# A fused transformer layer on one core: first attention with some transfers issued from ScalarE's queue, other buffers and another unit order

## The chip, the cores and the metric

The kernel runs on one core of a Trainium2 chip. The metric is the device time of one execution in microseconds. Below, PE is TensorE, PEld its weight loads, DVE VectorE, ACT ScalarE, POOL GpSimd, and SP SyncE, which in this kernel issues every DMA. A DMA is issued by an instruction in one engine's own queue and is done when its data has landed.

## What is computed

The reference is one transformer layer in float32 on 1024 tokens of width 1024: a feed-forward part, a token mixer, a second feed-forward part and a last norm. The change lies in the token mixer:

```
proj = h @ w_in                      # queries, keys, values, gates
y_da = diff_attention(q_da, k_da, v_da, ...)   # 8 heads, two components each
y_ns = nsa(q_ns, kc, vc, ks, vs, kw, vw, ...)  # 16 heads: compressed, selected, window
merged = sigmoid(g_a) * (y_da @ w_proj_da) + sigmoid(g_b) * (y_ns @ w_proj_nsa)
```

`diff_attention` rotates queries and keys, takes two causal softmaxes p0 and p1 of 64-wide components, forms a = p0 - lam * p1, multiplies by the 128-wide values of the head, and applies an RMS norm to each head's result.

## The kernel before, in words

Every matrix product of the projections is done with high and low halves: `split` (line 85) writes the rounded high half on ACT and the remainder on DVE, and `mm3` (line 48) does three matmuls, high by high, low by high, high by low.

`mix` (line 1107) calls `prelim` (line 1139), `da_phase` (line 1223) and `ns_phase` (line 1284). All three draw on **units**, generators of one projection each:

- `rope_pair` (line 531) makes a pair of 128-wide column blocks of queries or keys, both blocks of 512 tokens in turn (the index tb). It rotates them (tiles `m13`, `m42`), splits them into `rh` and `rl`, and stores them to DRAM scratch (line 553): queries as high, low, high, keys as high, low. The pool `mp` holds one buffer for each of these four tags.
- `v_da_unit` (line 561) makes the values of one head: gemm, transposes, split into `vh` and `vl`, two stores (line 576). `vh` takes the buffer of tag `rh`, `vl` that of `rl`.
- `cmp_block` (line 747) is the compressed attention; it runs for the second attention's queries inside the four units u = 0 to 3 at the end of `prelim`, and ends in the stores of line 780.

`prelim` makes the raw columns, compressed keys and values, values of heads 0 and 1, then the four units with `cmp_block`, and closes its pools. `da_phase` opens pools for keys `dk` (B_DK = 4 buffers), values `dv` and queries `dq` (4 buffers) and then drains six units: queries and keys of heads 0 and 1 (pair 0), then queries, keys and two value units of pair 1, with head 0's keys and values loaded between them by `da_load_parts` (line 900) and the first queries loaded before the last unit.

Then come 8 heads h with 4 steps m each. `da_queries` (line 801) loads the queries of a step: two tiles, four DMAs (line 808). `da_scores` (line 814) computes, for two 128-row blocks z of the step and both components c, the scores S (line 789; 128 (i + 1) columns for row block i = 2m + z), mask and row maximum on DVE (line 796), and the exponential into `Pt` on ACT (line 798). S has two buffers in PSUM. `finish` of the step before transposes and splits the weights (`tr_split`, tiles `th` and `tl`, line 844), multiplies by the values (`da_pv`, lines 866 to 868) and, for every second step, normalizes: `da_finish2` (line 880) works in tiles `yr` and `zr`, writes both halves `yo` of the result into the same two tags and stores them (line 893). A head's keys are two tiles `kt`, loaded at line 906, its values two tiles `vt`, line 913.

Beside the heads runs a **filler** (`Filler`, line 1030): the units of pairs 2 and 3, gate units and, in the second attention, output projections. After each row block `step` hands out its share of gemms; the weights are loaded at line 1055 and split at lines 1065 and 1066.

Each engine works through its own list in order. The lists are laid down when the kernel is built, from the program's order, which sets the priorities, and a simulated timeline (line 1564); a DMA issue stands in the list of the engine that issues it, and an instruction whose semaphore is not there yet holds all that stand behind it in that list.

Of the kernel before, what the change touches and what calls it, by code (L numbers as in the profile page):

```python
# [7 lines left out]
F32 = mybir.dt.float32  # L8
F32R = mybir.dt.float32r
# [521 lines left out]
def rope_pair(K, c, scr, cmp=None):  # L531
    nc = K.nc
    w = [load_w(K, K.A["win"][c]), load_w(K, K.A["win"][c + 1])]
    for tb in range(NTB):
# [17 lines left out]
        for hl, t in ((0, rh), (1, rl), (2, rh))[:scr.shape[0]]:  # L552
            nc.sync.dma_start(out=scr[hl].rearrange("a s d t -> (s d) a t")[:, :, sl], in_=t.bitcast(F32))
        if cmp is not None:
            uh = K.mq.tile([P, 2, TB], F32R, tag="uh", name="uh")
            ul = K.mq.tile([P, 2, TB], F32R, tag="ul", name="ul")
            split(nc, uh, ul, uf)
            cmp(tb, uh, ul)


def v_da_unit(K, h):
    nc = K.nc
    w = load_w(K, K.A["win"][C_VDA + h])
    for tb in range(NTB):
        ps = K.gm.tile([P, TB], F32, tag="gm", name="gm")
        yield from fill_gemm(K, ps, w, K.h[tb])
        vt = K.mp.tile([P, TB], F32, tag="m13", name="vt")
        nc.vector.tensor_tensor(out=vt, in0=ps, in1=K.R[tb], op=ALU.mult)
        tr = K.gm.tile([P, 4, P], F32, tag="gm", name="tr")
        for j in range(4):  # L570
            nc.tensor.transpose(tr[:, j], vt[:, j * P:(j + 1) * P], K.ident)
        vh = K.mp.tile([P, 4, P], F32R, tag="rh", name="vh")
        vl = K.mp.tile([P, 4, P], F32R, tag="rl", name="vl")
        split(nc, vh, vl, tr)
        for hl, t in ((0, vh), (1, vl)):
            nc.sync.dma_start(out=K.s_v[h][hl][:, tb * 4:tb * 4 + 4], in_=t.bitcast(F32))

# [222 lines left out]

def da_queries(K, h, m):
    nc = K.nc
    qt = []
    p, s0 = h // 2, (h % 2) * 2
    for c in range(2):
        t = K.qp.tile([P, 2, 2 * P], F32R, tag="q", name="qt")
        for z in range(2):
            nc.sync.dma_start(out=t[:, z].bitcast(F32),
                              in_=K.s_q[p][z:z + 2, :, s0 + c, :, m * 256:(m + 1) * 256].rearrange("h a d t -> (h a) d t"))
# [70 lines left out]
def da_finish2(K, h, H, ob, sq):  # L880
# [8 lines left out]
    nc.vector.scalar_tensor_tensor(out=ob, in0=ob, scalar=K.hgain[:, h:h + 1], in1=y, op0=ALU.mult, op1=ALU.mult)  # L889
    yo = [K.op.tile([P, TB], F32R, tag=t, name="yo") for t in ("yr", "zr")]  # L890
    split(nc, yo[0], yo[1], ob)
    for i in range(2):
        nc.sync.dma_start(out=K.s_yda[H][h][:, i], in_=yo[i].bitcast(F32))

# [244 lines left out]
def prelim(K, cg):  # L1139
    nc, A = K.nc, K.A  # L1140
    K.gm = open_pool(K, cg, "gm0", 4, True, side="right")
    with ExitStack() as ctx:
# [30 lines left out]
        with ExitStack() as c2:  # L1173
# [14 lines left out]
            drain([v_da_unit(K, 1)])  # L1188
        for u in range(4):
            drain([rope_pair(K, C_QNS + 2 * u, K.s_qns[u], lambda tb, uh, ul, u=u: cmp_block(K, u, tb, uh, ul))])  # L1190

# [14 lines left out]
B_ST = 2  # L1206
B_DK = 4
B_DV = 2
# [14 lines left out]
def da_phase(K, cg):  # L1223
    nc = K.nc
    with ExitStack() as ctx:
        K.kp, K.vp, K.qp = open_pool(K, ctx, "dk", B_DK), open_pool(K, ctx, "dv", B_DV), open_pool(K, ctx, "dq", B_DQ)
        K.nk, K.vv = {}, {}
        for n, f in enumerate(da_units(K, 0)[:2] + da_units(K, 1)):
            if n == 2:
                early = da_load_parts(K, 0)  # L1230
            if n >= 2:
                next(early)
            if n == 5:
                q0 = da_queries(K, 0, 0)
            drain([f()])
        cg.close()
        K.low = LOW_DA
# [28 lines left out]
        for p in range(4):  # L1266
            fill.pace(4 * (p + 1) if p < 2 else 8 + ng * (p - 1), PACE_DA)
            for h in (2 * p, 2 * p + 1):
                if h:
                    da_load(K, h)  # L1270
                for m in range(4):
                    qt = q0 if h + m == 0 else da_queries(K, h, m)
                    if h == 4:
                        ns_load_key(K, m)
                    res = da_scores(K, h, m, qt, fill.step)
                    if pend:
# [113 lines left out]
def body(tc, A, out):  # L1390
    nc = tc.nc
    K = Ctx()
    K.tc, K.nc, K.A = tc, nc, A
    K.low, K.vv, K.gate, K.fill, K.seen = 0, {}, None, None, {}
    K.h, K.acc, K.R = [None] * 2, [None] * 2, [None] * 2
# [173 lines left out]
```

## Time and profile before

| what | value |
|---|---|
| median of 3 runs | 2980.08 us (2974.42 to 2980.65) |
| the profiled execution's own time | 2971.48 us |
| its span, first to last instruction | 2969.7 us |
| mean granted TensorE clock | 0.992 of full speed |
| PE busy | 2860.9 us (96%) |
| DVE, ACT, POOL busy | 1981.6 (67%), 1268.5 (43%), 971.5 us (33%) |
| DMA | 478.19 MB, 161 GB/s, 46.5% of 16 engines' time, all from SP's queue |

By stage, in us from the span's start: first feed-forward part 0 to 650, `prelim` 650 to 980, first attention 980 to 1490, second attention 1490 to 2100, projections to 2230, second feed-forward part to the end.

How to read it: "busy" counts an instruction from start to end; matmuls overlap, so a stretch with PE busy throughout is fed, not necessarily at its peak. The number in square brackets at the end of a timeline row is the idle time just before it and what ended that. PEclk in a table of stretches is the granted clock, 1.00 for 2.4 GHz and 0.50 for 1.2 GHz.

### The profile page before, as it was taken

What the parts mean: (1) busy time and instruction counts of PE and PEld (TensorE: products, weight loads), DVE (VectorE), ACT (ScalarE), POOL (GpSimd) and SP (SyncE); (2) the same over time, 40 slices, a digit from 0 to 9 for tenths busy, and PEclk for the clock granted to TensorE, in tenths of its full rate; (3) what the DMA queues carried; (4) which work ended last, traced back from release to release, by engine and by line L of the source; (5) the groups of instructions that cost most, each with busy time, mean ns of one, the idle gap of its engine ahead of it and who ended that gap; (6) DMA issues with size and microseconds to landing.
All of it is one profiled execution on the core that took longest, in us unless ns stands there. A gap on an engine that the chain in (4) does not pass through costs nothing.

```text
span 2969.7 us, 39965 instructions
## 1 busy us (share of the span) xinstructions
PE 2860.9 (96%) x14238; PEld 2390.4 (80%) x14238; DVE 1981.6 (67%) x3140; ACT 1268.5 (43%) x2195; POOL 971.5 (33%) x765
## 2 busy tenths in 40 slices
PE   8999999999999899989899999999999999999998
PEld 6887887888788678778778888888878888788886
DVE  8765666666687467667677777776333866667656
ACT  6322234443233245445566666666432522223443
POOL 4356651000144123222333233333242435664101
PEclk9999999999999999999999999999999999999999
DMA  4345458655456544544332234222742245455854
GB/s 139 113 167 195 155 188 309 215 182 167 153 201 219 185 163 158 180 166 163 113 119 84 86 114 162 77 83 78 290 153 93 71 145 177 164 190 203 290 182 148
DMA packets 212710, 478.19 MB, mean 161 GB/s; under 512 B 20896, under 2 KB 39584, under 8 KB 212512
## 3 DMA queue, kind: packets, MB, share of 16 engines
q1 hardware_dynamic: 212512, 475.65, 46.5%
q8 instruction: 112, 1.84, 0.2%
q14 instruction: 86, 0.70, 0.1%
HBM read 313.56 MB, written 162.00 MB: 160 GB/s over the span
## 4 chain that ended last, share of the span: by engine, by line
PE 67%; DMA 10%; DVE 6%; issue 4%; ACT 3%; POOL 2%; SPq 1%; DVEq 0%; ACTq 0%; POOLq 0%
PE gm L49 6%; PE S L789 6%; PE gm L50 6%; PE gm L51 6%; PE Y L324 5%; PE acc L49 5%; PE acc L51 5%; PE acc L50 5%; PE tr L844 4%; PE Z L324 4%; PE X L324 3%; PE o L1002 2%; PE o L1001 2%; DMA sg<-smx 2%; DVE wlo L82 1%
## 5 line engine op out<-in xcount | busy, mean ns | idle before, releaser
L49 PE MATMUL gm<-hi,whi 128*128 128x512 f32 x880 | 351.3, 399 | 4.1 <-ACT whi L86 1.7
L51 PE MATMUL gm<-hi,wlo 128*128 128x512 f32 x880 | 347.7, 396 | 1.0 <-DVE wlo L82 1.0
L50 PE MATMUL gm<-lo,whi 128*128 128x512 f32 x880 | 348.0, 395 | 0.0
L789 PE MATMUL S<-kt,qt 128*128 128x320 f32 (+5 forms) x1152 | 275.3, 353 | 35.9 <-ACT Pt L798 11.3
L82 DVE TENSOR_TENSOR tl<-tr,th 128x512 fp32r<-128x512 f32 (+2 forms) x384 | 236.2, 619 | 88.1 <-ACT th L86 84.5
L86 ACT ACTIVATE th<-tr 128x512 fp32r<-128x512 f32 (+2 forms) x384 | 203.7, 542 | 197.4 <-PE tr L844 193.8
L82 DVE TENSOR_TENSOR wlo<-st,whi 128x1024 fp32r<-128x1024 f32 x154 | 198.7, 1308 | 116.9 <-ACT whi L86 116.1
L324 PE MATMUL Y<-tf,whi 128*128 128x512 f32 x864 | 269.9, 394 | 4.4 <-DVE c L367 1.8
L796 DVE CUSTOM_DVE_ANT_0 S<-S,slab 128x896 f32<-128x896 f32 (+7 forms) x320 | 224.5, 709 | 65.5 <-PE S L789 59.8
L49 PE MATMUL acc<-whi 128*128 128x512 f32 (+1 forms) x628 | 242.8, 387 | 3.8 <-DVE u L398 3.8
L50 PE MATMUL acc<-wlo,whi 128*128 128x512 f32 (+1 forms) x628 | 242.8, 387 | 0.0
L51 PE MATMUL acc<-whi,wlo 128*128 128x512 f32 (+1 forms) x628 | 242.7, 388 | 0.0
L86 ACT ACTIVATE whi<-st 128x1024 fp32r<-128x1024 f32 x154 | 160.3, 1057 | 192.4 <-PE acc L51 109.7
L955 POOL TENSOR_SCALAR Ps<-Ps,l 128x384 f32<-128x384 f32 (+7 forms) x128 | 100.8, 788 | 426.0 <-DVE l L953 212.6
L789 PEld LDWEIGHTS S<-kt,qt 128*128 128x128 f32 x1152 | 183.5, 190 | 60.7 <-ACT Pw L798 13.2
L82 DVE TENSOR_TENSOR wlo<-a,whi 128x1024 fp32r<-128x1024 f32 x90 | 136.6, 1522 | 96.4 <-ACT whi L86 96.3
L49 PEld LDWEIGHTS gm<-hi,whi 128*128 128x128 f32 x880 | 168.0, 191 | 37.1 <-issue 2.0
L51 PEld LDWEIGHTS gm<-hi,wlo 128*128 128x128 f32 x880 | 167.7, 191 | 37.5 <-DVE wlo L82 1.7
L324 PEld LDWEIGHTS Y<-tf,whi 128*128 128x128 f32 x864 | 161.3, 188 | 45.0 <-issue 4.2
L50 PEld LDWEIGHTS gm<-lo,whi 128*128 128x128 f32 x880 | 167.8, 191 | 30.8
L324 PE MATMUL Y<-tf,wlo 128*128 128x512 f32 x432 | 169.4, 393 | 0.0
L1001 PE MATMUL o<-th,vt 128*128 128x256 f32 (+1 forms) x608 | 164.4, 287 | 1.8 <-ACT th L86 1.7
(314 smaller groups left out, 7007.5 us busy)
## 6 DMA issues: line engine op xcount, KB each, us to landing
wst<-in_win_dram SPq DMA_DIRECT2D x55, 512.0 KB
sw<-w2s SPq DMA_DIRECT2D x44, 512.0 KB
st<-sw SPq DMA_DIRECT2D x88, 256.0 KB
st<-saT SPq DMA_DIRECT2D x88, 256.0 KB
a<-in_f1w_dram SPq DMA_DIRECT2D x36, 512.0 KB
a<-in_f2w_dram SPq DMA_DIRECT2D x36, 512.0 KB
st<-saB SPq DMA_DIRECT2D x66, 256.0 KB
qt<-sq SPq DMA_DIRECT2D x128, 128.0 KB
```

The costliest lines, as they stand in the source:

```text
L49: first = nc.tensor.matmul(out, lhsT=w[0][:, wk], rhs=x[0], start=start, stop=False, skip_group_check=skip)
L50: nc.tensor.matmul(out, lhsT=w[0][:, wk], rhs=x[1], start=False, stop=False, skip_group_check=skip)
L51: nc.tensor.matmul(out, lhsT=w[1][:, wk], rhs=x[0], start=False, stop=stop, skip_group_check=skip)
L82: return nc.vector.tensor_tensor(out=lo, in0=src, in1=hi.bitcast(F32), op=ALU.subtract)
L86: nc.scalar.activation(out=hi, in_=src, func=AF.Copy)
L324: K.mark = nc.tensor.matmul(o, lhsT=w[a][:, m * h + k], rhs=x[k][b], start=start and k == 0 and i == 0, stop=k == h - 1 and i == 2, skip_g ...
L789: K.last = nc.tensor.matmul(S[:, o:o + n], lhsT=q, rhs=k[:, k0 + c:k0 + c + n], start=i == 0, stop=i == 1)
L796: nc.vector.tensor_tensor_reduce(out=sv, in0=sv, in1=mv, scale=-0.125, scalar=BIG, op0=ALU.add, op1=ALU.min, accum_out=nm)
L844: nc.tensor.transpose(tr[:, b * P:(b + 1) * P], src, K.ident)
L955: nc.gpsimd.tensor_scalar(out=p[:, 0:n], in0=p[:, 0:n], scalar1=l[:, c:c + 1], scalar2=1.0, op0=ALU.mult, op1=ALU.mult)
L1001: nc.tensor.matmul(dst, lhsT=v, rhs=hi[:, b * P:(b + n) * P], start=False, stop=False, skip_group_check=True)
L1002: nc.tensor.matmul(dst, lhsT=v, rhs=lo[:, b * P:(b + n) * P], start=False, stop=last, skip_group_check=True)
```

## The change

- `rope_pair` issues the stores of the high half (hl 0 and 2) from ACT's queue, that of the low half stays on SP. This holds for all its callers.
- `v_da_unit` puts both halves into one tile of 4 KB per partition and takes the buffers of tags `rl`, `m42`, `rh` in turn (`K.vturn`); the high store goes to ACT's queue.
- `da_queries` takes the issuing engine as an argument. The loads of the first two steps are issued from SP before the head loop; those of step n + 2 from ACT, right after the scores of step n in program order. `dq` keeps 4 buffers.
- `da_finish2` writes the result's halves into own tiles `yh` and `yl`; the high store goes to ACT's queue. `dk` goes from 4 to 3 buffers.
- The query and key units of pair 0 move from the start of `da_phase` to `prelim`, ahead of unit u = 3. The four units of pair 1 stay in `da_phase`, with one part of head 0's keys and values loaded before each.

```diff
--- before.py
+++ after.py
@@ -550,12 +550,17 @@
         rl = K.mp.tile([P, 2, TB], F32R, tag="rl", name="rl")
         split(nc, rh, rl, m13)
         for hl, t in ((0, rh), (1, rl), (2, rh))[:scr.shape[0]]:
-            nc.sync.dma_start(out=scr[hl].rearrange("a s d t -> (s d) a t")[:, :, sl], in_=t.bitcast(F32))
+            (nc.sync if hl == 1 else nc.scalar).dma_start(out=scr[hl].rearrange("a s d t -> (s d) a t")[:, :, sl],
+                                                          in_=t.bitcast(F32))
         if cmp is not None:
             uh = K.mq.tile([P, 2, TB], F32R, tag="uh", name="uh")
             ul = K.mq.tile([P, 2, TB], F32R, tag="ul", name="ul")
             split(nc, uh, ul, uf)
             cmp(tb, uh, ul)
+
+
+def halves(t):
+    return t[:, 0], t[:, 1]
 
 
 def v_da_unit(K, h):
@@ -569,11 +574,11 @@
         tr = K.gm.tile([P, 4, P], F32, tag="gm", name="tr")
         for j in range(4):
             nc.tensor.transpose(tr[:, j], vt[:, j * P:(j + 1) * P], K.ident)
-        vh = K.mp.tile([P, 4, P], F32R, tag="rh", name="vh")
-        vl = K.mp.tile([P, 4, P], F32R, tag="rl", name="vl")
+        K.vturn += 1
+        vh, vl = halves(K.mp.tile([P, 2, 4, P], F32R, tag=("m42", "rh", "rl")[K.vturn % 3], name="vhl"))
         split(nc, vh, vl, tr)
         for hl, t in ((0, vh), (1, vl)):
-            nc.sync.dma_start(out=K.s_v[h][hl][:, tb * 4:tb * 4 + 4], in_=t.bitcast(F32))
+            (nc.scalar, nc.sync)[hl].dma_start(out=K.s_v[h][hl][:, tb * 4:tb * 4 + 4], in_=t.bitcast(F32))
 
 
 def v_ns_unit(K, br):
@@ -798,14 +803,13 @@
     return nc.scalar.activation(out=pv, in_=sv, func=AF.Exp, scale=-1.0, bias=nm, accum_out=l)
 
 
-def da_queries(K, h, m):
-    nc = K.nc
+def da_queries(K, h, m, eng):
     qt = []
     p, s0 = h // 2, (h % 2) * 2
     for c in range(2):
         t = K.qp.tile([P, 2, 2 * P], F32R, tag="q", name="qt")
         for z in range(2):
-            nc.sync.dma_start(out=t[:, z].bitcast(F32),
+            eng.dma_start(out=t[:, z].bitcast(F32),
                               in_=K.s_q[p][z:z + 2, :, s0 + c, :, m * 256:(m + 1) * 256].rearrange("h a d t -> (h a) d t"))
         qt.append(t)
     return qt
@@ -887,10 +891,10 @@
     z = K.op.tile([P, TB], F32, tag="zr", name="zr")
     newton_rsqrt(nc, y, z, m, nc.gpsimd)
     nc.vector.scalar_tensor_tensor(out=ob, in0=ob, scalar=K.hgain[:, h:h + 1], in1=y, op0=ALU.mult, op1=ALU.mult)
-    yo = [K.op.tile([P, TB], F32R, tag=t, name="yo") for t in ("yr", "zr")]
+    yo = [K.op.tile([P, TB], F32R, tag=t, name="yo") for t in ("yh", "yl")]
     split(nc, yo[0], yo[1], ob)
     for i in range(2):
-        nc.sync.dma_start(out=K.s_yda[H][h][:, i], in_=yo[i].bitcast(F32))
+        (nc.scalar, nc.sync)[i].dma_start(out=K.s_yda[H][h][:, i], in_=yo[i].bitcast(F32))
 
 
 def da_load(K, h):
@@ -1187,6 +1191,8 @@
             compress_fin(K, 1)
             drain([v_da_unit(K, 1)])
         for u in range(4):
+            if u == 3:
+                drain([f() for f in da_units(K, 0)[:2]])
             drain([rope_pair(K, C_QNS + 2 * u, K.s_qns[u], lambda tb, uh, ul, u=u: cmp_block(K, u, tb, uh, ul))])
 
 
@@ -1204,7 +1210,7 @@
 
 B_W = 2
 B_ST = 2
-B_DK = 4
+B_DK = 3
 B_DV = 2
 B_DQ = 4
 B_DP = 7
@@ -1225,14 +1231,12 @@
     with ExitStack() as ctx:
         K.kp, K.vp, K.qp = open_pool(K, ctx, "dk", B_DK), open_pool(K, ctx, "dv", B_DV), open_pool(K, ctx, "dq", B_DQ)
         K.nk, K.vv = {}, {}
-        for n, f in enumerate(da_units(K, 0)[:2] + da_units(K, 1)):
-            if n == 2:
-                early = da_load_parts(K, 0)
-            if n >= 2:
-                next(early)
-            if n == 5:
-                q0 = da_queries(K, 0, 0)
+        early = da_load_parts(K, 0)
+        for f in da_units(K, 1):
+            next(early)
             drain([f()])
+        steps = [(h, m) for h in range(8) for m in range(4)]
+        qts = [da_queries(K, *steps[i], nc.sync) for i in range(2)]
         cg.close()
         K.low = LOW_DA
         log_exp(K)
@@ -1269,10 +1273,11 @@
                 if h:
                     da_load(K, h)
                 for m in range(4):
-                    qt = q0 if h + m == 0 else da_queries(K, h, m)
                     if h == 4:
                         ns_load_key(K, m)
-                    res = da_scores(K, h, m, qt, fill.step)
+                    res = da_scores(K, h, m, qts.pop(0), fill.step)
+                    if h * 4 + m + 2 < len(steps):
+                        qts.append(da_queries(K, *steps[h * 4 + m + 2], nc.scalar))
                     if pend:
                         finish(*pend)
                     pend = (h, m, res)
@@ -1391,6 +1396,7 @@
     nc = tc.nc
     K = Ctx()
     K.tc, K.nc, K.A = tc, nc, A
+    K.vturn = 0
     K.low, K.vv, K.gate, K.fill, K.seen = 0, {}, None, None, {}
     K.h, K.acc, K.R = [None] * 2, [None] * 2, [None] * 2
     with ExitStack() as ctx:
```

## Rows read from the trace of the kernel before

**Rows 1.** The page, part 1: busy us, share of the span, instructions by engine.

```profile
PE 2860.9 (96%) x14238; PEld 2390.4 (80%) x14238; DVE 1981.6 (67%) x3140; ACT 1268.5 (43%) x2195; POOL 971.5 (33%) x765
```

**Rows 2.** Stretches: length, PE, PEld, DVE, ACT, POOL busy, PEclk, DMA, GB/s.

```profile
800.00:960.00 160.00, 160.00 (x828) 136.49 (x827) 129.08 (x191) 50.56 (x63) 74.77 (x56) 1.00 0.56 203
980.00:1490.00 510.00, 466.62 (x2397) 392.72 (x2398) 340.10 (x698) 235.56 (x480) 130.24 (x131) 0.96 0.47 163
1490.00:2100.00 610.00, 588.07 (x3762) 523.12 (x3761) 440.92 (x1132) 381.78 (x882) 187.56 (x259) 1.00 0.30 102
```

**Rows 3.** Stretches, as rows 2: five of the eight with the clock at 0.50.

```profile
980.57:990.81 10.24, 6.46 (x17) 5.06 (x18) 2.38 (x8) 0.92 (x4) 0.62 (x2) 0.50 0.59 223
1202.44:1205.85 3.41, 3.41 (x9) 2.64 (x8) 2.80 (x9) 2.03 (x4) 0.37 (x1) 0.50 0.25 103
1250.22:1253.63 3.41, 3.41 (x10) 2.65 (x9) 2.06 (x5) 3.06 (x6) 0.71 (x1) 0.50 0.45 167
1277.53:1284.35 6.82, 5.17 (x17) 4.49 (x18) 3.77 (x11) 3.48 (x9) 0.58 (x1) 0.50 0.26 100
...
1475.50:1482.33 6.83, 5.89 (x26) 5.60 (x27) 2.37 (x4) 3.35 (x7) 3.16 (x3) 0.50 0.01 2
```

**Rows 4.** PE's timeline, pauses: start, us, what [idle before, what ended it].

```profile
980.75 0.45 PE L789 MATMUL S<-kt,qt 128*128 128x128 f32 x1 [3.29 <-issue]
...
985.86 0.66 PE L789 MATMUL S<-kt,qt 128*128 128x128 f32 x2 [3.59 <-DMA kt<-sk]
...
1249.61 1.56 PE L789 MATMUL S<-kt,qt 128*128 128x512 f32 x4 [2.47 <-ACT Pt L798]
...
1279.18 1.22 PE L789 MATMUL S<-kt,qt 128*128 128x512 f32 x2 [4.59 <-ACT Pt L798]
...
1476.30 0.58 PE L866 MATMUL o<-th,vt 128*128 128x256 f32 x1 [2.52 <-ACT th L86]
```

**Rows 5.** Waits of PE, 980 to 1490: us in total, times, longest.

```profile
PE S L789 <- ACT Pt L798: 11.3, 9, 4.6
PE o L866 <- ACT th L86: 6.9, 3, 4.1
...
PE S L789 <- DMA qt<-sq: 2.0, 3, 0.9
```

**Rows 6.** Waits of ACT, 960 to 1480, as rows 5.

```profile
ACT whi L1065 <- DMA wst<-in_win_dram: 14.6, 2, 7.8
...
ACT vh L86 <- DMA sk<-rh: 8.2, 2, 4.6
ACT yr L117 <- DMA syd<-yo: 8.1, 1, 8.1
ACT vh L86 <- DMA sv<-vh: 4.5, 1, 4.5
```

**Rows 7.** Waits of SP's queue, 940 to 1460, as rows 5.

```profile
SPq L808 <- PE S L789: 89.8, 28, 8.7
...
SPq L906 <- DMA sk<-rl: 8.6, 1, 8.6
```

**Rows 8.** DMA issues: count: least, median, most ns on SP; first, last.

```profile
L808 SPq DMA_DIRECT2D qt<-sq x128: 509/537/4852, 948.1 to 1437.9; - x128
...
L893 SPq DMA_DIRECT2D syd<-yo x32: 319/380/4425, 1086.0 to 1504.4; - x32
```

**Rows 9.** PE's timeline, scores at two changes of head, columns as rows 4.

```profile
1262.47 0.42 PE L789 MATMUL S<-kt,qt 128*128 128x128 f32 x2
...
1413.70 2.08 PE L789 MATMUL S<-kt,qt 128*128 128x512 f32 x8
...
1421.33 0.44 PE L789 MATMUL S<-kt,qt 128*128 128x128 f32 x2 [1.25 <-ACT Pt L798]
```

**Rows 10.** The chain that ended last: start, us, what was waited for.

```profile
973.32 11.69 DMA kt<-sk
...
1289.97 7.61 DMA vt<-sv
```

## The prediction

> **What bounds the kernel now.** I read the page's busy times first, then a table of stretches by stage, the clock, PE's timeline for its pauses, and last the waits of the engines that ended those. PE is busy 96% of the span [rows 1], so nothing can be won but PE's pauses and what the lowered clock costs. By stage they are uneven [rows 2]: the last part of `prelim` has no pause, the first attention pauses 510.00 - 466.62 = 43.4 us, the second 21.9. A measurement here can tell about 0.2% from no change; the first attention's pauses are seven times that.
>
> The clock fell from 2.4 to 1.2 GHz in eight stretches between 980 and 1490, each behind a pause of PE or beginning in one; five of them are [rows 3]. In such a stretch PE does half of what it would, so half of its busy time there is lost as well. The longest pauses [rows 4] share one trait. The first scores waited for a key load (3.29 + 3.59 us). The pauses of 2.47 and 4.59 us are put down to ACT's exponential, but ACT itself stood at `vh`, waiting until a store out of that buffer had landed [rows 6]. The 2.52 us at 1476 are ACT held 8.1 us at `yr` by the stores of `yo` [rows 6]; a pause of 4.1 us [rows 5] is ACT held at a weight split for a load [rows 6]. So ACT waits for stores and loads that all pass through SP's queue, and SP's queue stood 89.8 us, 28 times, at query loads whose buffer the scores had not yet freed [rows 7].
>
> **The change part by part.** The sum is made on the profiled execution, 2971.48 us with a span of 2969.7. The median is 8.60 us above it; I carry the difference over to the median.
>
> Unit order. The key load of head 0 stood 8.6 us for the store of pair 0's last low keys [rows 7] and then took 11.69 us with three others [rows 10]. With pair 0 moved ahead of the whole unit u = 3 that store has long landed. What is late next is the memory: the pools `dk` and `dq` lie where `prelim`'s pools were, so the load waits for the last of `cmp_block`, now behind it; the four units of pair 1 cover that with gemms. At stake are 6.9 us of pause and 6.46 / 2 = 3.2 us of clock [rows 3, 4], 10.1 in all. Bounds 0 and 10.1; a loss is excluded as far as those gemms suffice. PE's list is fixed at build time and the first scores were evidently placed before the real landing; that may come again, so I take 6.0. In `prelim` itself PE is fed throughout [rows 2], so moved gemms cost nothing there.
>
> Buffers of the values. The two pauses fall in value units 4 and 5. Counting `K.vturn`, their first halves take `m42` (which only POOL reads, no store) and `rl`, whose last store lies two value halves back. The pauses of 7.1 us go, and with them (3.41 + 5.17) / 2 = 4.3 us of clock [rows 3, 4]: 11.4. Unit 2 takes `rl` right behind a store of `rl`, so that wait of ACT stays; the trace shows no pause put down to it. I take 10.5, bounds 5 and 11.4.
>
> Own tiles `yh`, `yl`. ACT's 8.1 us at `yr` happened once, at the seam to the second attention, and cost 2.5 us of pause and 5.89 / 2 = 2.9 us of clock [rows 3, 4]. The query loads of the second attention pause PE just before it, so the clock may fall anyway: 4.0 of 5.4, bounds 2 and 5.4.
>
> Query loads off SP. PE's waits for queries, 2.0 us, and the 4.1 us pause behind a late weight load [rows 5], with 3.41 / 2 = 1.7 us of clock [rows 3], sum to 7.8. Depth does not grow: before, too, four buffers let a load go as soon as the scores two steps back were done, which is what SP waited for [rows 7]. What grows is the freedom of weights, keys, values and low stores behind it on SP. I take 4.0, bounds 0 and 7.8.
>
> Issues on ACT. Of 128 query loads 8 stay on SP and 120 go to ACT, at a median of 537 ns: 64 us. High stores in the stretch, some 45 (queries, keys, values, results), at the 380 ns of a result's store [rows 8]: 17 us. No row shows a DMA issued from ACT, so SP's durations stand for it. ACT goes from 235.6 us to about 317 of 510, 62%; the cover is its idle time of 274 us. Each group of four loads holds ACT 4 x 0.537 = 2.1 us, and behind it stand exponentials and `th`, for which PE waits. The loads need the scores of their step finished, which the exponential behind them needs as well, so the wait itself adds little. From below: a stretch with ACT at 381.8 of 610, 63%, has 21.9 us of pauses in all [rows 2], or 18.3 per 510; of the present 43.4 only 11.3 + 6.9 - 2.47 - 4.59 - 4.1 - 2.52 = 4.5 us are waits for ACT that no transfer explains [rows 4, 5]. Between the two lie 0 to 14 us, and I take 6.0, nearer the present stage, since not every pause of the later one need be ACT's. The far end: every group fully on the path, 30 x 2.1 = 64 us. A gain below nothing is excluded: the issues are only moved onto a longer list. The store issues in `prelim` (some 28 more) lie in ACT's idle time, 50.6 busy of 160, under a PE that is never short [rows 2].
>
> Three key buffers. The next head's first component still loads a head ahead; its second now waits for the last scores of the current first component. At 1249.61 to 1251.2 those scores end and the new head's second component begins at 1262.47, 11.3 us later [rows 4, 9]: a load of 7.61 us, as of values of the same 512 KB [rows 10], fits. Where the filler has run thin, the scores end near 1413.70 + 2.08 / 2 = 1414.7 and it begins at 1421.33, 6.6 us later [rows 9]: 1.5 us short with 0.5 us to issue, at two changes of head, plus clock. I take 3.0; bounds 0 and, with 11.69 us for every load and all seven changes, about 16.
>
> Sum: 6.0 + 10.5 + 4.0 + 4.0 - 6.0 - 3.0 = 15.5 us less: 2971.5 becomes 2956.0, and on the median 2980.08 - 15.5 = 2964.6.
>
> **Weighed against a rule.** The rows show transfers landing late, 7.6 us for values and 11.7 for keys [rows 10], on one queue. The Trainium skill (DMA: Bandwidth & Descriptors, section Issuing engines are not separate DMA queues) says that DMAs begun from several engines run on the same 16 DMA engines and that starting them elsewhere only saves the sequencer's time. By that rule the term of the query loads would be nothing and stores would land no sooner. The trace has one queue only, so no run here shows yet whether it holds; the sum by the rows is 15.5 us less, by the rule that of the second rival.
>
> **The rivals.** *All of it pays.* ACT's idle time covers the issues and keys arrive: 10.1 + 11.4 + 5.4 + 7.8 = 34.7 us, 2945. For it: ACT is idle half of the stage. Against: groups of issues come in bursts. Chance 0.15.
>
> *Only the buffers pay.* Transfers land as late as before because the DMA engines, not the queue, are what they wait for. Then 10.5 + 4.0 remain, less 9.0 for ACT and keys: 5.5 less, 2974.6. For it: landing times are several times an issue. Against: SP's long stand in front of the scores [rows 7]. Chance 0.17.
>
> *ACT becomes what PE waits for: slower.* Each group of query loads stands before an exponential. If a full queue stretches issues as on SP (most 4852 ns [rows 8]), or if the build's order puts the group in front of `th`, each costs PE 1.2 us (half a group, and some clock): 30 x 1.2 = 36 instead of 6, so 14.5 more: 2994.6. It decides from (15.5 + 6.0) / 30 = 0.7 us of PE per group. For it: ACT held 4.5 us made PE pause 4.59 [rows 4, 6]. Against: two score buffers, and fillers that can run meanwhile. Chance 0.15.
>
> *It doesn't do what it says:* the loads are no deeper, as said; that is in the forecast, not apart.
>
> **How the numbers follow.** The forecast has 0.53. The range reaches from the first rival, 2945, to 2985, which takes in the second and the nearer part of the third, and 3 us further at both ends, half of what the three runs lie apart; outside are the rest of the third and gains beyond the sum. So it is 2942 to 2988. Faster by over 0.2% is below 2974.1: most of the forecast's 0.53, the first rival's 0.15, and near a fifth of the second: 0.68. Within 0.2%: 0.15. Slower: the third and a little of the forecast's spread: 0.17.
>
> **What would show it.** Right: in the first attention PE's pauses fall from 43 to some 25 us and the clock's stretches from eight to four or five; no wait of ACT for `sv`, `sk` or `syd`; SP's wait for the scores gone; ACT's own issues near 0.54 us. The key step is wrong if PE waits for `kt` at the changes of head, the order step if it still does at the first scores. The whole is wrong if PE's waits for `Pt` and `th` pass 25 us, or if the time changes outside 900 to 1500.

## The result, and the profile after

The changed kernel is slower: a median of 3015.95 us in four runs beside 2979.82 us of the kernel before, a ratio of 1.0138 with a 95% interval of 1.0123 to 1.0152, or 41 us more. The forecast was 15.5 us less, with a range that ended at 2988. The profiled execution has a span of 3020.1 us, 50.4 us above that of before.

The page of the changed kernel, busy times and DMA queues (packets, MB, share of 16 engines):

```profile
PE 2878.9 (95%) x14238; PEld 2402.7 (80%) x14238; DVE 1983.2 (66%) x3140; ACT 1270.1 (42%) x2195; POOL 976.4 (32%) x765
...
q1 hardware_dynamic: 180640, 429.51, 41.8%
q10 hardware_dynamic: 31872, 46.14, 4.3%
```

Beside [rows 1], every engine does the same instructions in about the same time; q10, ACT's queue, is new. The stretches of the changed kernel, columns as [rows 2]:

```profile
650.00:980.00 330.00, 324.74 (x1618) 273.12 (x1617) 228.02 (x341) 99.86 (x137) 86.22 (x66) 1.00 0.52 176
980.00:1490.00 510.00, 438.34 (x2157) 364.76 (x2156) 308.79 (x637) 211.99 (x432) 123.39 (x119) 0.92 0.45 152
1490.00:2100.00 610.00, 583.41 (x3697) 517.22 (x3696) 441.08 (x1128) 378.44 (x873) 186.69 (x255) 0.99 0.31 103
```

All of the loss lies in the first attention. Of 510 us PE pauses 510.00 - 438.34 = 71.7 us, against 43.4 before [rows 2], 28 more. The mean clock falls from 0.96 to 0.92 of full speed; with levels of 1.00 and 0.50 that is 0.16 x 510 = 82 us at the low level instead of 41, and half of the 41 us added, at most, is lost work. Together 28 + 20 = 48 us of the 50. The last scores of the first attention run at 1511.5 us, 51 later than before.

What ended PE's pauses, 900 to 1540 in the changed kernel (us in total, times, longest):

```profile
PE S L794 <- ACT Pt L803: 29.4, 14, 5.6
PE S L794 <- DMA kt<-sk: 16.5, 3, 7.3
PE tr L576 <- DVE vt L573: 5.2, 3, 4.6
PE S L794 <- DMA qt<-sqn: 4.8, 2, 2.8
PE S L794 <- ACT whi L1069: 4.8, 1, 4.8
PE o L870 <- ACT th L86: 4.1, 4, 1.5
```

The waits for `Pt` went from 11.3 [rows 5] to 29.4 us, those for keys from 3.6 to 16.5. ACT does no more work than before, so what held it is in its own waits, same stretch:

```profile
ACT Pt L803 <- DMA qt<-sq: 21.2, 5, 7.9
ACT Pt L803 <- issue: 15.6, 2, 9.8
ACT rh L86 <- DMA sq<-rh: 14.6, 2, 8.8
```

The first row is odd. An exponential doesn't read `qt`; its scores do. The chain of the changed kernel shows how it comes to wait for one (start, us, what; two pieces, in order of time):

```profile
1324.76 16.54 DMA qt<-sq
1341.38 0.52 ACTq L812
1342.00 0.56 ACT Pt L803
1343.04 3.35 PE S L794 x8
...
1406.53 19.91 DMA qt<-sq
1426.46 0.51 ACTq L812
1427.02 0.57 ACT Pt L803 x2
```

A query load issued at 1324.76 took 16.5 us to land. Only then did ACT *issue* the next load, and only behind that stood the exponential that freed the scores' buffer; PE paused 5.59 us. The trace's semaphores say why ACT stood: the load of 1341.38 counts on the same semaphore as that of 1324.76 (SP and ACT share eight for all their DMAs), and in this program an issue waits until the DMA before it on its semaphore has landed; by my count of the semaphore updates all 1425 issues of the trace that have one before them do. At the median the issues as such are as short as forecast, 517 ns (line L812; count: least, median, most ns):

```profile
L812 ACTq DMA_DIRECT2D qt<-sq x120: 514/517/7071, 1019.2 to 1489.2; - x120
```

The most, 7.07 us, is no single case: 15 of the 120 took over 0.6 us, 29.5 us together. Some of the stores issued from ACT stretch too; one of the two cases in the row of waits that ends in "issue" is such a store. ACT's timeline around it, and PE's (start, us, what, idle before and what ended it):

```profile
1212.61 5.40 ACTq L553 DMA_DIRECT2D sq<-rh  x1
...
1219.46 1.11 ACT L803 ACTIVATE Pt<-S,nm 128x1024 f32<-128x1024 f32 x1 [5.79 <-issue]
...
1220.72 0.69 PE L794 MATMUL S<-kt,qt 128*128 128x128 f32 x2 [5.08 <-ACT Pt L803]
```

So ACT was held in two ways, by the wait for an earlier landing and by issues that themselves took microseconds. Two things are left to explain: why 128 KB take 16 us to land, and what each part of the change adds.

### The profile page after: what moved, and what is told of

It reads as the page before. It is cut to its first block, busy times and chain, and to the rows that moved or that the text cites. A ratio compares the mean times of both kernels' runs of the same rounds, so it can differ in the third digit from the quotient of the medians.

```text
span 3020.1 us, 39926 instructions
## 1 busy us (share of the span) xinstructions
PE 2878.9 (95%) x14238; PEld 2402.7 (80%) x14238; DVE 1983.2 (66%) x3140; ACT 1270.1 (42%) x2195; POOL 976.4 (32%) x765
## 4 chain that ended last, share of the span: by engine, by line
PE 45%; DMA 4%; DVE 3%; issue 2%; ACT 2%; POOL 1%; SPq 0%; ACTq 0%; DVEq 0%; POOLq 0%
PE S L794 5%; PE tr L848 3%; PE Y L324 3%; PE gm L49 3%; PE gm L51 3%; PE gm L50 3%; PE Z L324 2%; PE X L324 2%; PE acc L49 2%; PE acc L51 2%; PE acc L50 2%; PE o L1006 2%; PE o L1005 2%; DMA qt<-sq 1%; PE po L50 1%
## 5 line engine op out<-in xcount | busy, mean ns | idle before, releaser
L794 PE MATMUL S<-kt,qt 128*128 128x320 f32 (+5 forms) x1152 | 277.8, 354 | 66.2 <-ACT Pt L803 29.4
```

Source lines behind the costliest of these rows:

```text
L794: K.last = nc.tensor.matmul(S[:, o:o + n], lhsT=q, rhs=k[:, k0 + c:k0 + c + n], start=i == 0, stop=i == 1)
```

## The experiments

Ratios are to the kernel before on the same chip, with 95% intervals; before's medians were 2972.3, 2973.6, 2973.3 and 2974.9 us in the four sets. Landing times that no row shows are my count of the semaphore updates in the traces, loads issued between 980 and 1460 us.

### Parts taken back out of the changed kernel

Query loads on SP again:

```diff
-qts.append(da_queries(K, *steps[h * 4 + m + 2], nc.scalar))
+qts.append(da_queries(K, *steps[h * 4 + m + 2], nc.sync))
```

> The changed kernel with the query loads of step n + 2 issued from SP again; all else as changed. Theory A (ACT's issues hold ACT, and the exponentials behind them hold PE): 30 us or more come back, at or below 2986 us, and PE's waits for Pt fall from 29.4 us to under 15 in the first attention. Theory K (three key buffers: the second component's keys land late at the changes of head): under 12 us come back, about 3005, and the waits for kt stay at 16 us. Theory O (the unit order): about 3010 to 3016, no change.

All stores on SP again:

```diff
-            (nc.sync if hl == 1 else nc.scalar).dma_start(out=scr[hl].rearrange("a s d t -> (s d) a t")[:, :, sl],
+            nc.sync.dma_start(out=scr[hl].rearrange("a s d t -> (s d) a t")[:, :, sl],
...
-            (nc.scalar, nc.sync)[hl].dma_start(out=K.s_v[h][hl][:, tb * 4:tb * 4 + 4], in_=t.bitcast(F32))
+            nc.sync.dma_start(out=K.s_v[h][hl][:, tb * 4:tb * 4 + 4], in_=t.bitcast(F32))
...
-        (nc.scalar, nc.sync)[i].dma_start(out=K.s_yda[H][h][:, i], in_=yo[i].bitcast(F32))
+        nc.sync.dma_start(out=K.s_yda[H][h][:, i], in_=yo[i].bitcast(F32))
```

> The changed kernel with all stores issued from SP again; the query loads stay on ACT. Theory A with the query loads as the cost: within 6 us of the changed kernel, 3010 to 3022, since some 45 stores at about 0.4 us hold ACT 17 us in all. If the stores are what holds ACT: 20 us or more come back, below 2996. Theories K and O: 3010 to 3022.

Four key buffers, and the result's halves in `yr` and `zr` again:

```diff
-B_DK = 3
+B_DK = 4
...
-    yo = [K.op.tile([P, TB], F32R, tag=t, name="yo") for t in ("yh", "yl")]
+    yo = [K.op.tile([P, TB], F32R, tag=t, name="yo") for t in ("yr", "zr")]
```

> The changed kernel with four key buffers and the result's halves in yr and zr again, which is what the memory allows. Theory K: the three waits for kt, 16.5 us, go, with some 13 us of clock, so 2986 to 2996. Theory A: under 12 us come back, 3004 to 3014, and the waits for Pt stay near 29 us. Theory O: no change.

Pair 0's units back in `da_phase`:

```diff
-            if u == 3:
-                drain([f() for f in da_units(K, 0)[:2]])
...
-        early = da_load_parts(K, 0)
-        for f in da_units(K, 1):
-            next(early)
+        for n, f in enumerate(da_units(K, 0)[:2] + da_units(K, 1)):
+            if n == 2:
+                early = da_load_parts(K, 0)
+            if n >= 2:
+                next(early)
```

> The changed kernel with the units of pair 0 at the start of the first attention again. Theory O: 20 us or more come back, below 2996. Theories A and K: within 8 us, 3008 to 3024.

| kernel | median us | ratio | interval | against 1.0138 |
|---|---|---|---|---|
| query loads on SP | 3008.97 | 1.0123 | 1.0108 to 1.0138 | about 4 us less, not told apart |
| stores on SP | 3001.59 | 1.0100 | 1.0085 to 1.0115 | 11 us less |
| 4 key buffers, `yr`, `zr` | 2998.40 | 1.0090 | 1.0075 to 1.0105 | 14 us less |
| old unit order | 3005.25 | 1.0104 | 1.0087 to 1.0121 | 10 us less |

No single part is the culprit, and none shows as a gain. Nor does any theory get what it expected: A's 30 us from the query loads and O's 20 us from the order did not come, K's 2996 was missed by 2 us, and the stores gave more than the 6 us and less than the 20 that were expected of them. With the query loads back on SP ACT's waits at `Pt` for query loads fall from 21.2 to 6.5 us, but PE's time goes elsewhere; its waits, 900 to 1540:

```profile
PE S L794 <- DMA kt<-sk: 26.7, 5, 9.7
PE S L794 <- ACT Pt L803: 16.1, 5, 4.9
```

Keys take the place of exponentials. Whatever is moved, some transfer is late.

### Parts put alone into the kernel before

Three key buffers:

```diff
-B_DK = 4
+B_DK = 3
```

> The kernel before with three key buffers and nothing else. Theory K: waits of PE for kt come in at the changes of head, 15 to 28 us with their clock, so 0.5 to 1.0% slower. Rival (the key load is late only because the other edits crowd the queues): within 0.2% of before.

Query loads issued from ACT, at their old place in the program:

```diff
-            nc.sync.dma_start(out=t[:, z].bitcast(F32),
+            (nc.scalar if h + m else nc.sync).dma_start(out=t[:, z].bitcast(F32),
```

> The kernel before with 120 of its 128 query loads issued from ACT, called at the same place in the program, and nothing else. Theory A: 10 to 20 us slower, with PE's waits for Pt at 20 us or more, up from 11.3. Theory K: within 5 us, since SP's queue gets shorter and the keys have four buffers.

(The text says 120; the edit moves 124, all but the four of the first step.)

Value halves in one tile, in three buffers in turn, stores on SP (`halves` and the start of `K.vturn` as in the change):

```diff
-        vh = K.mp.tile([P, 4, P], F32R, tag="rh", name="vh")
-        vl = K.mp.tile([P, 4, P], F32R, tag="rl", name="vl")
+        K.vturn += 1
+        vh, vl = halves(K.mp.tile([P, 2, 4, P], F32R, tag=("m42", "rh", "rl")[K.vturn % 3], name="vhl"))
```

> The kernel before with the value halves in one tile that takes the three buffers in turn, both stores on SP, and nothing else. The prediction's term: 5 to 11 us faster, no wait of ACT for sv and none of more than 1 us for sk at vh. Rival (another wait takes their place, since each build lays its lists anew): within 5 us.

The unit order alone (the diff of the old order above, the other way round; the first queries are loaded ahead of the last unit, as before):

> The kernel before with the units of pair 0 ahead of unit u = 3 and nothing else. The prediction's term: 0 to 10 us faster, the first scores without a wait for kt. Rival from the run that undid it: some 10 us slower, with PE waiting longer ahead of the first scores and at the stores of pair 1's queries.

Three key buffers, and query loads two steps ahead, all on SP:

```diff
-B_DK = 4
+B_DK = 3
...
-            if n == 5:
-                q0 = da_queries(K, 0, 0)
...
+        steps = [(h, m) for h in range(8) for m in range(4)]
+        qts = [da_queries(K, *steps[i]) for i in range(2)]
...
-                    qt = q0 if h + m == 0 else da_queries(K, h, m)
...
-                    res = da_scores(K, h, m, qt, fill.step)
+                    res = da_scores(K, h, m, qts.pop(0), fill.step)
+                    if h * 4 + m + 2 < len(steps):
+                        qts.append(da_queries(K, *steps[h * 4 + m + 2]))
```

> The kernel before with three key buffers and the query loads placed two steps ahead in the program, all on SP, old layout. Theory E: queries of the step after next now go ahead of the key load that the same scores release, 512 KB on the same four engines, so PE waits for kt at five or more changes of head, 15 to 30 us, and the kernel is 10 to 25 us slower; three key buffers alone cost 2. Rival: as with three key buffers alone, within 5 us of before.

The stores of high halves issued from ACT, as the change does it and nothing else (the three lines shown above for stores on SP, the other way round):

> The kernel before, only the stores of high halves (of queries, keys, values, results) issued from ACT's queue. Theory (what ACT pays is standing at an issue for an earlier landing, and stores take turns with loads on the engines): +4 to +12 us, since taking these stores back out of the changed kernel gave 11 us; ACT has waits at the lines of the stores of some us each, and PE pauses for exponentials or splits behind them. Rival (only the query loads cost, and the stores' share in the changed kernel came from the two together): -3 to +3 us. The prediction's step costed some 45 issues of the stretch at 380 ns each, 17 us on ACT, nearly all beside other work: +0 to +2 us.

| kernel | median us | ratio | interval | forecast |
|---|---|---|---|---|
| 3 key buffers | 2975.94 | 1.0009 | 0.9999 to 1.0018 | +3.0 us |
| query loads on ACT | 2998.89 | 1.0081 | 1.0066 to 1.0096 | -4.0 for SP, +6.0 for ACT with the stores |
| value buffers | 2974.54 | 1.0000 | 0.9990 to 1.0009 | -10.5 us |
| unit order | 2982.75 | 1.0029 | 1.0018 to 1.0040 | -6.0 us |
| 3 key buffers, queries ahead on SP | 2990.50 | 1.0050 | 1.0032 to 1.0067 | no term of its own |
| high stores on ACT | 2978.87 | 1.0014 | 1.0002 to 1.0025 | in the +6.0 |

Three key buffers, value buffers and the unit order came out as the rivals in their texts had it; the query loads cost more than theory A's 20 us; queries ahead cost what theory E had, though at three changes of head and not five; the high stores came out at the low end of their theory, with an interval that reaches into the rival's +3.

**Query loads on ACT** are the largest part: 0.0081 x 2973.6 = 24 us. PE's waits for `Pt` go from 11.3 to 19.3 us:

```profile
PE S L789 <- ACT Pt L798: 19.3, 8, 7.0
```

ACT's timeline of that kernel (start, us, what, idle before and what ended it):

```profile
1310.58 0.53 ACTq L808 DMA_DIRECT2D qt<-sq  x1
...
1311.24 0.62 ACT L117 ACTIVATE yr<-m 128x512 f32<-128x512 f32 x1
1323.00 0.52 ACTq L808 DMA_DIRECT2D qt<-sq  x1
1323.56 0.63 ACT L118 ACTIVATE yr<-yr 128x512 f32<-128x512 f32 x1 [11.70 <-DMA qt<-sq]
...
1324.10 0.88 ACT L798 ACTIVATE Pt<-S,nm 128x768 f32<-128x768 f32 x1
```

and PE's:

```profile
1325.13 1.11 PE L789 MATMUL S<-kt,qt 128*128 128x448 f32 x2 [6.97 <-ACT Pt L798]
```

From 1311.9 to 1323.0 ACT stood at one issue, whose semaphore had last been given to a query load of 1298.86; that one landed at 1322.98, 24 us after its issue. The exponential of 1324.10 stood behind it and PE paused 6.97 us. By my count query loads land in 7.0 us at the median and 16.6 at the ninth tenth, with SP's queue 7.6 and 12.8: from the second queue they come no sooner, and the late ones later.

**Value buffers.** The two pauses of 7.1 us that the forecast took out are gone (waits for `Pt` fall to 4.6 us), and the time is the same. PE's waits of that kernel, 900 to 1540, and its stretch, columns as [rows 2]:

```profile
PE o L870 <- DMA vt<-sv: 7.3, 1, 7.3
PE S L793 <- DMA qt<-sq: 6.7, 5, 4.3
...
PE S L793 <- ACT Pt L802: 4.6, 6, 1.2
...
980.00:1490.00 510.00, 463.29 (x2398) 389.82 (x2396) 340.44 (x694) 234.63 (x475) 131.49 (x131) 0.96 0.47 162
```

With `vt` at 2.8 and `qt` at 2.0 us before, 4.5 + 4.7 us of new waits for transfers stand where 6.7 us of waits for `Pt` went, and the mean clock stays at 0.96. Whether these transfers are late because of the pauses taken out, or because the build laid its lists anew, was not tried.

**Unit order.** PE's timeline and ACT's wait (960 to 1100) of that kernel:

```profile
1009.71 0.80 PE L49 MATMUL gm<-hi,whi 128*128 128x512 f32 x1 [9.08 <-ACT whi L86]
```

```profile
ACT rh L86 <- DMA sq<-rh: 26.3, 2, 18.5
```

The first scores, at 1010.7, have no pause for keys any more, only 2.6 us for queries. But ACT stands 18.5 us at `rh`, because the store of the queries before it is not out of that buffer, and a weight split stands behind it: one pause of 9.08 us in front of the first scores in place of 6.9 us at them. By my count that store was issued at 979.9 and landed at 998.7, right behind two key loads that landed at 990.4 and 996.3.

**Key buffers.** Three alone make PE pause for keys at the last two changes of head, where the forecast had put it:

```profile
1373.62 0.41 PE L789 MATMUL S<-kt,qt 128*128 128x128 f32 x2 [3.45 <-issue]
1421.29 0.66 PE L789 MATMUL S<-kt,qt 128*128 128x128 f32 x2 [3.94 <-DMA kt<-sk]
```

The first is put down to "issue", but by my count the second component's key landed at 1373.5, just before it. (PE's waits for `kt` add up to 8.2 us, of which 4.2 are at the very first scores, as before.) With queries two steps ahead the wait for `kt` is:

```profile
PE S L789 <- DMA kt<-sk: 23.7, 5, 9.1
```

Of these 3.4 us are at the first scores and 19.9 at three changes of head. The scores that free the key's buffer free the query loads' as well. SP's timeline of the changed kernel with its queries on SP shows it at the last change of head:

```profile
1445.55 2.57 SPq L812 DMA_DIRECT2D qt<-sq  x4
1448.17 0.51 SPq L910 DMA_DIRECT2D kt<-sk  x1
```

The key's buffer was free at 1445.5; four query loads of a step that is not due for long went ahead of it.

### What the transfers wait for

Two microseconds of the changed kernel in the middle of the landing of 16.5 us, columns as [rows 2]:

```profile
1338.00:1340.00 2.00, 0.00 (x0) 0.00 (x0) 0.00 (x0) 0.00 (x0) 0.00 (x0) 1.00 0.26 88
```

Nothing computes, everything waits for transfers, and the DMA engines are at 0.26 of what they could do. A quarter is no accident: of the first 198 stretches of two microseconds from 980 on, 57 of the kernel before and 55 of the changed one have a share of 0.23 to 0.28. The semaphores of the traces name the loads: a query or key load, of either attention, posts five updates, one about 1 us after its issue begins and four when data lands; the other loads and stores of the trace post sixteen. So these loads run on 4 of the 16 engines. The Trainium skill (DMA: Bandwidth & Descriptors, section Why a DMA increments its semaphore by 16 and not by 1) says that a DMA takes the largest number of engines, up to 16, that divides the slowest dimension of both of its sides, and that the sequencer posts the rest at once. The pattern `"h a d t -> (h a) d t"` has 4 groups of 32 rows in DRAM and 128 partitions in SBUF; by that rule 4, and the trace agrees.

If these four engines are the bound, spreading the loads must win what no shuffling of queues did. The scratch gets a layout in which the 128 rows of a load lie at one stride, and a pair's store is cut in four by rows. The scratch of keys and of the second attention, the query loads and the second attention's loads are edited in the same way as the lines shown:

```diff
-        K.s_q = [dr.tile([3, 2, 4, 32, T], F32, name=f"sq{p}") for p in range(4)]
+        K.s_q = [dr.tile([4, 3, 2, 32, T], F32, name=f"sq{p}") for p in range(4)]
...
-            nc.sync.dma_start(out=scr[hl].rearrange("a s d t -> (s d) a t")[:, :, sl], in_=t.bitcast(F32))
+            for s in range(4):
+                nc.sync.dma_start(out=scr[s, hl].rearrange("a d t -> d a t")[:, :, sl],
+                                  in_=t[s * 32:(s + 1) * 32].bitcast(F32))
...
-        nc.sync.dma_start(out=t.bitcast(F32), in_=K.s_k[p][:, :, s0 + c].rearrange("h a d t -> (h a) d t"))
+        nc.sync.dma_start(out=t.bitcast(F32), in_=K.s_k[p][s0 + c].rearrange("h a d t -> (h a d) t"))
```

in the kernel before,

> The kernel before with the scratch of queries and keys laid out so that a load's 128 rows follow one another at one stride; each store of a pair is cut in four by rows. Theory E (a load whose rows come in 4 groups of 32 runs on 4 of the 16 DMA engines, and those four are what the loads queue for): 8 to 25 us faster, PE's waits for qt, vt and kt gone, landings of query loads near 4 us. Rival (the engines are not what the loads queue for): within 5 us, or slower by the 3 x 40 added store issues at 0.4 us on SP.

in the changed kernel,

> The changed kernel with the same layout and cut stores. Theory E: what the change lost comes back for the most part: within 8 us of b_spread, at or below 2975 us on the scale where before has 2973. Theory A (the issues themselves hold ACT): still 20 us or more slower than b_spread, since ACT issues as many loads and more stores than in the changed kernel.

and in the kernel before with its query loads on ACT:

> The kernel before with the new layout and the query loads issued from ACT. Theory E: within 6 us of b_spread, where the same edit in the old layout cost 24 us. Theory A: 15 to 25 us slower than b_spread.

That edit touches layout, stores and the second attention's loads at once. The last one leaves these alone and only cuts each query and key load of the first attention into four loads of 32 rows (the key loads in the same way):

```diff
-        for z in range(2):
-            nc.sync.dma_start(out=t[:, z].bitcast(F32),
-                              in_=K.s_q[p][z:z + 2, :, s0 + c, :, m * 256:(m + 1) * 256].rearrange("h a d t -> (h a) d t"))
+        for z in range(2):
+            for g in range(4):
+                nc.sync.dma_start(out=t[g * 32:(g + 1) * 32, z].bitcast(F32),
+                                  in_=K.s_q[p][z + g // 2, g % 2, s0 + c, :, m * 256:(m + 1) * 256])
```

> The kernel before, each query and key load of the first attention cut into four loads of 32 rows; DRAM layout, stores and the second attention's loads untouched. A load of 32 rows at one stride is expected to run on all 16 engines. Theory (the four engines that these loads share are the bound): most of the 41 us that the new layout took out of the first attention comes back, -25 to -42 us, ratio 0.986 to 0.992; the stretches of two microseconds with a DMA share near 0.26 go from 57 of 198 to under 15, and PE's pauses in the first attention fall from 46 to under 25 us. It costs SP 384 + 48 more issues, 432 x 0.3 to 0.5 = 130 to 220 us of a list that mostly waits. Rival A (the gain of the layout came from the stores cut in four, or from where the rows lie in DRAM): no gain, 0 to +10 us for the issues. Rival B (issues on SP become the bound): shares fall as in the theory, but weights and values land later behind 32 issues a step, -10 to +10 us.

| kernel | median us | ratio | interval |
|---|---|---|---|
| before, new layout | 2924.10 | 0.9837 | 0.9815 to 0.9858 |
| changed, new layout | 2925.64 | 0.9837 | 0.9816 to 0.9859 |
| before, query loads on ACT, new layout | 2921.93 | 0.9827 | 0.9806 to 0.9847 |
| before, loads cut in four | 2940.99 | 0.9891 | 0.9864 to 0.9917 |

Stretches of the kernel before with the new layout:

```profile
980.00:1490.00 510.00, 495.35 (x2677) 420.79 (x2677) 383.16 (x801) 268.65 (x556) 155.49 (x160) 1.00 0.53 171
```

and two microseconds of it (the view's share can pass 1.00; before the change it reaches 1.36 in one such stretch):

```profile
1268.00:1270.00 2.00, 2.00 (x14) 1.75 (x13) 0.99 (x2) 0.00 (x0) 1.73 (x4) 1.00 1.08 386
```

Its DMA issues (last column: median us to landing):

```profile
qt<-sq SPq DMA_DIRECT2D x128, 128.0 KB, 2.6
...
kt<-sk SPq DMA_DIRECT2D x16, 512.0 KB, 4.9
```

The pauses of the stretch fall from 43.4 to 14.7 us and the clock stays up. Query loads land in 2.6 us where my count gives 7.6 before, keys in 4.9 instead of 13.8. The stretches near 0.26 fall from 57 to 5, and those above 0.90 rise from 28 to 44. The 49 us are far above the 8 to 25 expected, and come with 204 more store issues by my count, not 120. The cut of the loads alone, with layout and stores as they were and 432 issues more, gives 32 of these 49 us, inside its theory's range. Each cut load posts sixteen updates; the stretches near 0.26 are 20:

```profile
980.00:1490.00 510.00, 483.97 (x2565) 409.29 (x2564) 369.52 (x769) 257.70 (x534) 150.21 (x154) 0.98 0.53 171
```

Two of its signs were just missed: 20 such stretches instead of under 15, and pauses of 26.0 us instead of under 25 (the 46 named there for before are the 43.4 of [rows 2]).

So most of the gain comes from taking the loads off their four engines, and not from the stores or from where rows lie. Transfers that use all 16 engines land sooner with it: the high stores of values, which neither edit touches, in 2.2 us at the median with the cut and 2.4 with the new layout, against 6.7 before, the filler's weights in 4.3 and 5.0 against 8.8. That a part of each stood behind the loads on those four engines fits this; no run shows it for one engine by itself. By PE's last scores of the first attention, 1460.5 us before, the cut kernel is 32.1 us ahead and the one with the new layout 40.5; another 8 us come in the second attention, whose loads had the same pattern. What makes the other 8 us of the first (issues saved, or the second attention's first loads, which the cut left on four engines) was not tried.

With the new layout the change costs nothing and wins nothing: both kernels stand at 0.9837. And the 24 us of query loads from ACT are gone: 0.9827 and 0.9837, intervals overlapping. PE's waits for `Pt` of that kernel:

```profile
PE S L791 <- ACT Pt L800: 3.5, 5, 0.8
```

A query issue on ACT takes 0.76 us there at most, against 5.22 in the old layout. So it is not the short issue that cost, but standing at it for a late landing or through a stretched one, and that only where PE needs what stands behind: in the changed kernel with the new layout ACT still waits some 62 us for landings between 900 and 1540, and PE only 3.7 us for `Pt`.

## Why the prediction was wrong

**The bound.** The step that failed first is "So ACT waits for stores and loads that all pass through SP's queue". The waits were read rightly, the resource was not: late landings came for the most part from loads that crowd four DMA engines, not from one engine's list; spreading the loads alone took 32 us off, shuffling queues nothing. The forecast's one row on it, keys in 11.69 us against 7.61 for values of the same size [rows 10], held a hint, as did the share of 0.25 and 0.26 in two rows of [rows 3]; the stage's mean share of 0.47 [rows 2] hid it. Every gain in the sum rested on a transfer or buffer coming free sooner, and none of these loads came sooner: the query loads land in 7.9 us at the median in the changed kernel, 7.6 before.

**Unit order, -6.0: measured +9 by itself, +5 to +12.** "A loss is excluded as far as those gemms suffice" failed: what is late next was not the memory of the pools but the queries' store out of `rh`, with weight splits behind it on ACT, and that store landed behind key loads. Taking it out of the changed kernel gave 10 us back, the same.

**Value buffers, -10.5: measured 0, -3 to +3.** The mechanism was right, the pauses went; that a pause taken out is time won was wrong: later transfers, `vt` and `qt`, take its place. That the four engines make them late is likely by the runs above, but the value buffers were not run alone with the new layout.

**Own tiles, -4.0.** Never run alone. Going back to `yr` and `zr` together with four key buffers gave 14 us, so whatever they won is less than what the keys cost; how much stays open.

**Query loads off SP and issues on ACT, -4.0 and +6.0: +24 for the loads, +4 for the stores.** The issue was priced at 0.537 us and measured 0.517 at the median, but 84 us in all instead of 64 in the changed kernel, because some are stretched; about half of that ran under an activation. What the step left out is in "the wait itself adds little": it had only the scores in mind and not the wait for the DMA before on a shared semaphore. Per group of four loads the run alone lost 24 / 31 = 0.8 us, just past the 0.7 from which the slower rival decides. The stores cost 4 us alone and 11 within the change; why more there stays open.

**Three key buffers, +3.0: measured +2.3 alone, 0 to +5**, at the changes of head that were named. The term missed what the change does beside it: with queries two steps ahead it is 0.0050 x 2973 = +15, measured with both on SP.

The single parts that were run alone add up to 9 + 0 + 24 + 4 + 2 = 39 us, and the change measured 41. That the two agree so well is partly luck: the parts are not independent, the own tiles are not among them, and three key buffers with queries ahead cost 15 instead of 2.

**The rivals.** "Only the buffers pay" had the right reason, that transfers land as late as before "because the DMA engines, not the queue, are what they wait for", with the wrong consequence: 5.5 us less, since buffers did not pay either. The rule weighed there (the Trainium skill, DMA: Bandwidth & Descriptors, section Issuing engines are not separate DMA queues) agrees with the landing times of the query loads moved alone, 7.0 us at the median against 7.6; by it the term of the query loads would have been nothing, and it says nothing of what stands behind an issue on ACT. "ACT becomes what PE waits for" came out in kind; its condition, that issues stretch as on SP, came true for 15 of 120, but its 14.5 us were too few because it had ACT's issues alone and no loss from order and keys. **The signs** given served: waits for `Pt` and `th` are 29.4 + 4.1 = 33.5 us, past the 25 that were to mark the whole as wrong; PE waits for `kt` at changes of head; the clock's low stretches between 980 and 1490 rose from eight to eleven; the time changed inside 900 to 1500 only. Also right: SP's wait for the scores at query loads [rows 7] is gone, ACT's waits for `sv` too, and those for `sk` and `syd` fell to 3.7 and 1.6 us.

## What to carry to other kernels

When transfers are late while the mean DMA share is moderate, look at it in stretches of microseconds. Here it stuck at a quarter, and the count of semaphore updates named the loads that ran on 4 of 16 engines. As long as they did, no other queue, order or buffer helped; each only chose which transfer was late. Giving a load's 128 rows one stride in DRAM took out 49 us, cutting the loads alone 32. And a DMA issue on a computing engine can cost far more than its half microsecond: it holds all that stands behind it in that engine's list for as long as it waits for an earlier landing or is itself stretched, here up to 11.1 and 7.1 us.

## What the runs showed of the hardware that was not expected

- A second queue shares the same engines, and not by need. While ACT stood at its issue, 1318 to 1324 of the kernel with query loads on ACT, the share was 0.26 throughout. By my count of the packets that ended in each two microseconds, SP's queue had 32, 40 and 51, some 130 KB each time, and ACT's 33, 39 and 52, 32 to 50 KB. Query packets are 1 KB there, SP's 4 or 2 KB; the two queues look served packet by packet, so the queue of small packets, whose data is due first, comes off worse. The Trainium skill (DMA: Bandwidth & Descriptors, section Queues, rings and completion order) says that each engine goes round the queues that have work, one packet at a time; the equal counts agree. No run changed the packet size to test it.
- A load at one stride is issued faster, too. Line L810 of the kernel before with the new layout, least, median and most ns, against 537 at the median before [rows 8]:

```profile
L810 SPq DMA_DIRECT2D qt<-sq x128: 319/422/1172, 952.3 to 1397.1; - x128
```
